# Hybrid attention layers: weighted sums with the exponentials as stationary operand, gates among the neighbourhood heads, earlier loads for scan and Fourier mixer

## The chip, the cores and the metric

One core of a Trainium2 chip runs the whole program. The metric is device microseconds of one execution. Three runs of the kernel before took 3113.3, 3114.28 and 3123.29 us, median 3114.28 us.

## The reference

Two layers act on 1024 latent tokens and 256 context tokens of width 1024. A layer normalises and modulates the tokens, projects them by one matrix `w_in`, feeds four head groups in parallel, joins their outputs (256 channels each) by one matrix `w_out`, and ends with a squared-ReLU MLP. The second layer gives no context output. The parts that matter here:

```python
# grouped-query attention (4 query heads, 2 key heads, 64 channels); scores and sums in float32
s = einsum('bqkgd,bskd->bkgqs', q, k_all)         # k_all: latent and context keys
o = einsum('bkgqs,bskd->bqkgd', softmax(s), v_all)
# neighbourhood attention (4 heads): an 8 x 16 window of the 16 x 64 grid with a bias, plus all context keys
p = softmax(concat([q.k_window + bias, q.k_ctx]))
o = p_window @ v_window + p_ctx @ v_ctx
# S5: two complex diagonal scans per group of 16 channels, then
t = gelu(y);  o = t * sigmoid(t @ w_glu)
# Fourier mixer: real part of a 2-D DFT over positions and channels, then
o = f @ w_fnet + b_fnet
y = concat([oa, ob, on, od]) @ w_out
```

## The kernel before, in words

Tokens stand in ten tiles of 128. Large projections are exact to float32 by three products of rounded halves (`mm3`, lines 159 to 161: high by high, high by low, low by high); scores and weighted sums are float32 products. The program is written in stages as Python generators, and `weave`, `every` and `along` interleave their steps; a scheduler then puts instructions into each engine's queue by priority, which `early` raises for side work. So the order in a queue follows from the steps' places and priorities. Each queue is worked in order.

A layer's attention (`attention`) runs over units: six for grouped-query attention (two key heads; four, four and two query tiles; the last are context queries and are absent in layer 1), then four neighbourhood heads. `gqa_main` and `na_main` take one tile of 128 keys after the other: PE makes scores (L641, L772), DVE adds the bias in neighbourhood heads (L153), ACT takes the exponential `e`, and two steps later `pv` (L611) makes the weighted sums. There v, with a column of ones, is the stationary operand (128 keys by 65 columns), and up to 512 queries of `e` stream past it; the result is 65 rows by queries, whose last row is the softmax denominator. At the end of a unit ACT copies the 64 rows to `oraw` and DVE copies the denominator row to `rden`; `finish` sends that row by DMA to a tile of 128 partitions (L665), takes the reciprocal (L671), sends it through DRAM (L672) back to 64 partitions (L675), and POOL multiplies `oraw` by it into `o`.

Among these steps runs side work: every second step one of the S5 scan `s5_scan` during the grouped-query units, every third step one of the Fourier mixer `fnet` during the neighbourhood heads, and `attn_prep` (queries, keys and maxima of the next unit). `s5_scan` loads three tables per group in the same step as the first product that reads them (L1268), and in its second group loads `t0` and copies it whole to `tm`, which ACT does in one instruction.

After the heads comes `w_out`. It loads eight 128-row units of `w_out` into `raw` tiles, splits each into `wh` and `wl`, splits the attention output into `oh` and `ol`, and makes products `wh,oh`. In its first steps it also runs `glu`, the gates of S5 (L1334 to L1369: loads of the scan's output `yt` and of `gwr`, GELU on DVE, ACT and POOL, products `th,gwh`, and a sigmoid times the input).

## Time and profile before

| | |
|---|---|
| median of three runs | 3114.28 us |
| profiled execution, its own time | 3110.25 us |
| its span, first to last instruction | 3108.5 us |
| mean granted TensorE clock | 0.968 |
| busy: PE, PEld, DVE, ACT, POOL | 93%, 76%, 53%, 35%, 30% |
| chain that ended last | PE 56%, DVE 6%, DMA 5% |
| `mm3` products of the w_in and MLP stages, largest group | 519.7 us (1536 products) |
| one of the weighted sums' groups (L611, `e,zg`) | 170.7 us (336 records) |

A clock of 1.0 is 2.4 GHz, and 0.5 is 1.2 GHz. Attention begins at 299.8 us in layer 0 and at 1956.6 us in layer 1 (first scores); its neighbourhood heads begin at 501.7 and 2160.3 us. The first product of the output projection stands at 670.43 and 2297.50 us. PE, the engine that is busy most, sets the pace nearly everywhere, so PE's waits and PE's own instructions are what to read; a float32 product shows as two records in the trace, each with its own weight load on PEld.

### The profile page before, as it was taken

How to read it: one execution, taken by the hardware profiler on the slowest of the kernel's cores; microseconds unless marked ns; L12 is line 12 of the kernel's file. 1: busy time of each engine (PE TensorE's matmuls, PEld its weight loads, DVE VectorE, ACT ScalarE, POOL GpSimd, SP SyncE). 2: the span in 40 equal slices, each digit the busy share in tenths (PEclk: the TensorE clock that was granted, in tenths of full speed). 3: DMA queues.
4: the chain of work that ended last, by engine and by line, in shares of the span. 5: the costliest groups of instructions: out<-in, count | busy, mean ns of one | idle time of the engine just before them, and what ended most of it. 6: DMA issues, size and time to landing. Idle time of an engine off the chain costs nothing.

```text
span 3108.5 us, 38660 instructions
## 1 busy us (share of the span) xinstructions
PE 2899.1 (93%) x14816; PEld 2361.5 (76%) x14816; DVE 1640.4 (53%) x2240; ACT 1094.7 (35%) x1856; POOL 938.2 (30%) x847
## 2 busy tenths in 40 slices
PE   6999897979999999999999989788979999999998
PEld 3788554658888889898988788554657888888887
DVE  3475564664775544754554785464755233443334
ACT  3443653553322222422222344454553222122212
POOL 2563222235521112511122563122335111111113
PEclk8999898979999999999999999998989999999999
DMA  7544425342544322432333443525343211111113
GB/s 280 171 129 108 95 72 152 84 158 82 176 149 130 128 90 82 158 120 95 116 102 109 152 141 104 94 72 147 96 156 113 64 55 41 54 41 55 54 41 109
DMA packets 244190, 340.04 MB, mean 109 GB/s; under 512 B 52037, under 2 KB 188581, under 8 KB 244005
## 3 DMA queue, kind: packets, MB, share of 16 engines
q1 hardware_dynamic: 244004, 337.57, 35.9%
q8 instruction: 116, 1.90, 0.3%
q14 instruction: 70, 0.57, 0.1%
HBM read 283.78 MB, written 53.62 MB: 109 GB/s over the span
## 4 chain that ended last, share of the span: by engine, by line
PE 56%; DVE 6%; DMA 5%; issue 3%; POOL 3%; ACT 2%; SPq 0%; DVEq 0%; POOLq 0%; ACTq 0%
PE ps L159 17%; PE ps L161 17%; PE ps L160 17%; PE ps L611 2%; DMA raw<-in_w_ada_dram 1%; DVE wl L150 1%; DVE y L153 1%; PE ps L772 1%; POOL rs L215 1%; PE ps L641 1%; DMA raw<-in_w_mlp_dram 0%; DVE acc L292 0%; DMA s5u<-u 0%; DVE y L1390 0%; DMA kd<-zn 0%
## 5 line engine op out<-in xcount | busy, mean ns | idle before, releaser
L159 PE MATMUL ps<-mh,wh 128*128 128x320 f32 (+1 forms) x1536 | 519.7, 338 | 11.5 <-DVE y L153 6.4
L147 ACT ACTIVATE wh<-raw 128x1024 fp32r<-128x1024 f32 x234 | 242.9, 1056 | 787.6 <-PE ps L161 551.9
L161 PE MATMUL ps<-mh,wl 128*128 128x320 f32 (+1 forms) x1536 | 517.5, 337 | 1.1 <-DVE wl L150 1.1
L160 PE MATMUL ps<-ml,wh 128*128 128x320 f32 (+1 forms) x1536 | 517.6, 337 | 0.0
L159 PE MATMUL ps<-wh,hidh 128*128 128x512 f32 x1152 | 451.5, 392 | 1.4 <-DVE y L153 1.4
L161 PE MATMUL ps<-wh,hidl 128*128 128x512 f32 x1152 | 447.8, 390 | 1.8 <-POOL hidl L150 1.8
L160 PE MATMUL ps<-wl,hidh 128*128 128x512 f32 x1152 | 449.3, 390 | 0.0
L153 DVE TENSOR_TENSOR y<-ps,y 128x1024 f32<-128x1024 f32 (+1 forms) x253 | 306.4, 1218 | 261.7 <-PE ps L161 261.7
L150 POOL TENSOR_TENSOR hidl<-r,hidh 128x640 fp32r<-128x640 f32 (+1 forms) x128 | 188.9, 1476 | 672.7 <-DVE r L153 672.7
L150 DVE TENSOR_TENSOR wl<-raw,wh 128x1024 fp32r<-128x1024 f32 x188 | 289.1, 1550 | 163.3 <-ACT wh L147 158.9
L159 PEld LDWEIGHTS ps<-mh,wh 128*128 128x128 f32 x1536 | 290.3, 189 | 37.4 <-issue 7.3
L161 PEld LDWEIGHTS ps<-mh,wl 128*128 128x128 f32 x1536 | 289.8, 189 | 22.3 <-DVE wl L150 2.3
L160 PEld LDWEIGHTS ps<-ml,wh 128*128 128x128 f32 x1536 | 290.3, 189 | 20.8
L150 POOL TENSOR_TENSOR wl<-raw,wh 128x1024 fp32r<-128x1024 f32 x48 | 120.3, 2507 | 471.6 <-ACT wh L147 471.5
L159 PEld LDWEIGHTS ps<-wh,hidh 128*128 128x128 f32 x1152 | 216.6, 188 | 52.2 <-issue 6.2
L161 PEld LDWEIGHTS ps<-wh,hidl 128*128 128x128 f32 x1152 | 216.5, 188 | 48.1 <-POOL hidl L150 2.7
L160 PEld LDWEIGHTS ps<-wl,hidh 128*128 128x128 f32 x1152 | 216.7, 188 | 43.2
L153 DVE TENSOR_TENSOR r<-r 128x640 f32<-128x640 f32 (+1 forms) x128 | 96.6, 755 | 241.7 <-ACT hidh L1488 241.6
L1486 ACT ACTIVATE r<-ps 128x640 f32<-128x640 f32 (+1 forms) x128 | 82.2, 644 | 367.9 <-PE ps L161 360.2
L611 PE MATMUL ps<-e,zg 128*65 128x512 f32 (+1 forms) x336 | 170.7, 598 | 3.8 <-DVE rden L653 2.8
L292 DVE SCALAR_TENSOR_TENSOR acc<-raw,cst,acc 128x1024 f32<-128x1024 f32 x70 | 101.5, 1474 | 136.1 <-DMA raw<-in_w_ada_dram 136.1
L159 PE MATMUL ps<-hh,wh 128*128 128x320 f32 (+1 forms) x480 | 151.5, 316 | 2.7 <-ACT vst L147 2.7
(427 smaller groups left out, 5328.1 us busy)
## 6 DMA issues: line engine op xcount, KB each, us to landing
raw<-in_w_mlp_dram SPq DMA_DIRECT2D x192, 512.0 KB
raw<-in_w_ada_dram SPq DMA_DIRECT2D x96, 512.0 KB
raw<-in_w_in_dram SPq DMA_DIRECT2D x28, 512.0 KB
x<-x SPq DMA_DIRECT2D x26, 512.0 KB
x<-h SPq DMA_DIRECT2D x18, 512.0 KB
x<-in_x_dram SPq DMA_DIRECT2D x16, 512.0 KB
raw<-in_w_out_dram SPq DMA_DIRECT2D x16, 512.0 KB
bq<-in_na_bq_dram SPq DMA_DIRECT2D x8, 800.0 KB
```

What stands on the lines that cost most here:

```text
L147: self.nc.scalar.activation(out, in_, AF.Copy, scale=scale)
L150: (eng or self.nc.vector).tensor_tensor(out=out, in0=a, in1=b, op=OP.subtract)
L153: (eng or self.nc.vector).tensor_tensor(out=out, in0=a, in1=b, op=op)
L159: self.nc.tensor.matmul(ps, ah, bh, start=start and i == 0, stop=False)
L160: self.nc.tensor.matmul(ps, ah, bl, start=False, stop=False)
L161: self.nc.tensor.matmul(ps, al, bh, start=False, stop=stop and i == n - 1)
L215: nc.gpsimd.tensor_tensor(out=r, in0=r, in1=self.mhalf.to_broadcast([128, n]), op=OP.pow)
L292: nc.vector.scalar_tensor_tensor(acc[c], x, col, acc[c], op0=OP.mult, op1=OP.add)
L611: self.nc.tensor.matmul(po[0:65], vf[:, kt, :], e, start=start, stop=stop)
L641: nc.tensor.matmul(ps, kk[:, ks], qq[:, hs], start=kk is k1, stop=kk is k2)
L772: nc.tensor.matmul(ps, kk[:, ks], qq[:, x:y], start=kk is k1, stop=kk is k2)
L1486: nc.scalar.activation(r.rearrange("p (b n) -> p b n", b=nb), ps[:, :nb, :w], AF.Relu)
```

## The change

**Weighted sums.** `e` becomes the stationary operand, 128 keys by 128 queries, and the 65 columns of v stream past it; the result is 128 queries by 65. Each query tile of each key tile is a product of its own: 1,088 of them in the program, where there were 304 products. `sums` first clears the two result banks with one-row bf16 products of zeros, 36 in all. The denominator now stands beside its sums on the same partition, so `divide` takes a reciprocal and multiplies on DVE; `finish` transposes the quotients on PE (72 transposes) and copies them into `o`. The copies `oraw` and `rden`, the three DMAs of each of 18 units, the way through DRAM and POOL's multiplications are gone. In neighbourhood heads, tiles that begin at an odd row of the grid are padded by 64 columns of zeros (POOL), and the sums of the context queries stand after the first key tile instead of at the head's end.

**Gates.** `glu` is chained behind `fnet` as side work among the neighbourhood heads, where a step of it now comes every 5/2 steps; `w_out` loads its eight units in one go and takes them in the order 0, 1, 2, 3, 6, 7, 4, 5.

**Loads.** `s5_scan` loads its tables one group ahead and `t0` three steps ahead of the first group, and copies `tm` in four parts; `fnet` loads four `u0` tiles at its start.

```diff
+        self.zero = c.tile([1, 512], BF16, name="zero")
+        nc.vector.memset(self.zero, 0.0)
...
-    def pv(self, queue, vf, kt, parts, start, stop):
+    def sums(self, n):
+
+
+        po = self.ps2(tag="pO")
+        for b in range(2):
+            self.nc.tensor.matmul(po[:, b * 512:b * 512 + n * 65], self.zero[:, :128], self.zero[:, :n * 65],
+                                  start=True, stop=False)
+        return po
+
+    def pv(self, queue, vf, kt, po, parts, end=()):
 
 
         def whole():
-            for po, e in parts:
-                self.nc.tensor.matmul(po[0:65], vf[:, kt, :], e, start=start, stop=stop)
+            for (b, c), e in parts:
+                self.nc.tensor.matmul(po[:, b * 512 + c * 65:b * 512 + c * 65 + 65], e, vf[:, kt, :],
+                                      start=False, stop=(b, c) in end)
         queue.append((2, whole))
...
+        po = self.sums(u["n"])
...
-            self.pv(queue, vf, kt, [(po[:, h * 512:h * 512 + w], e[:, h * w:(h + 1) * w]) for h in range(2)],
-                          kt == kts[0], kt == NT - 1)
+            self.pv(queue, vf, kt, po, [((h, t), e[:, h * w + t * 128:h * w + (t + 1) * 128])
+                                        for h in range(2) for t in range(u["n"])],
+                    [(h, u["n"] - 1) for h in range(2)] if kt == NT - 1 else ())
...
-        tags = (("oraw2", 256), ("rden2", 512)) if u["b"] == 2 else (("oraw", TOK), ("rden", TOK))
-        oraw, rden = (st["fp"].tile([128, n], F32, tag=tag, bufs=1, name=tag) for tag, n in tags)
-        for h in range(2):
-            self.copy(oraw[64 * h:64 * h + 64, :w], po[0:64, h * 512:h * 512 + w])
-        nc.vector.tensor_copy(rden[0:1, :2 * w].rearrange("p (h n) -> p h n", h=2),
...
+        n = u["n"]
+        on = st["fp"].tile([128, 4, 2, 64], F32, tag="on", bufs=2, name="on")
+        self.divide(st, po, on[:, :n].rearrange("p t h d -> p h t d"), n)
+        st["fin"] = self.finish(lambda t: on[:, t].rearrange("p h d -> p (h d)"), n, o, u["j"], u["t0"])
...
+    def divide(self, st, po, dst, n):
+
+        src = po.rearrange("p (b c) -> p b c", b=2)[:, :, :n * 65].rearrange("p b (t d) -> p b t d", d=65)
+        r = st["fp"].tile([128, 2, 5], F32, tag="rt", bufs=2, name="rt")[:, :, :n]
+        self.nc.vector.reciprocal(r, src[:, :, :, 64])
+        self.tt(dst, src[:, :, :, 0:64], r[:, :, :, None].to_broadcast([128, 2, n, 64]), OP.mult)
+
+    def finish(self, src, n, o, kt, t0):
+
+        yield
+        yield
+        for i0 in range(0, n, 4):
+            m = min(4, n - i0)
+            ps = self.ps1()
+            for i in range(m):
+                self.nc.tensor.transpose(ps[:, i * 128:(i + 1) * 128], src(i0 + i), self.ident)
+            for i, k, dst in self.put_o(o, kt, (t0 + i0) * 128, m * 128):
+                self.copy(dst, ps[:, i:i + k])
...
+        po = self.sums(nq // 256)
...
+            r0 = ra - ra % 2
+            e = st["pg"].tile([128, 1024], F32, tag="e", bufs=4, name="e")[:, :(rb - r0) * 64]
+            if r0 < ra:
+                nc.gpsimd.memset(e[:, 0:64], 0.0)
...
-            cols = [(po[:, x:y], slice(x - ra * 64, y - ra * 64)) for x, y in pieces]
-            self.pv(queue, s["vf"], kt, [(x, e[:, c]) for x, c in cols], i == 0, i == 9)
-            yield
+            self.pv(queue, s["vf"], kt, po, [((t % 2, t // 2), e[:, t * 128 - r0 * 64:(t + 1) * 128 - r0 * 64])
+                                             for t in range(r0 // 2, rb // 2)], [(0, 3), (1, 3)] if i == 9 else ())
+            yield
+            if i == 0 and nq > NLAT:
...
+                for c in range(2):
+                    ks = slice(1024 + c * 128, 1152 + c * 128)
+                    nc.tensor.matmul(ps[:, c, :], k1[:, ks], q1[:, 1024:1280], start=True, stop=False)
+                    nc.tensor.matmul(ps[:, c, :], k2[:, ks], q2[:, 1024:1280], start=False, stop=True)
...
+        if h % 2 == 0:
+            st["on"] = st["fp"].tile([128, NT, 2, 64], F32, tag="onn", bufs=1, name="onn")
+        on = st["on"]
+        n = nq // 256
+        self.divide(st, po, on[:, :2 * n, h % 2].rearrange("p (c b) d -> p b c d", b=2), n)
+        st["fin"] = iter(())
+        if h % 2:
+            st["fin"] = self.finish(lambda t: on[:, t].rearrange("p h d -> p (h d)"), 2 * n, o, 4 + h // 2, 0)
...
-                side, every = fnet, 3
+                side, every = fnet, 5 / 2
...
+        done = 0
         for i, x in enumerate(main):
-            if i % n == n - 1:
+            if int((i + 1) / n) > done:
+                done += 1
                 next(other, None)
             yield x
...
+            us = {}
+            for t0 in (0, 512, 256, 768):
+                us[t0] = p.tile([128, 516], F32R, tag="wh", bufs=4, name="u0")[:, :512].bitcast(F32)
+                nc.sync.dma_start(us[t0].rearrange("p (m t) -> p m t", m=2), uf[:, :, t0:t0 + 256])
...
+                if t0 not in us:
+                    nc.sync.dma_start(u, uf[:, :, t0:t0 + 256])
...
-        def front(g):
-            v, cs, sn = (p.tile([128, 2, w], F32, tag=n, bufs=2, name=n) for n, w in (("v", 128), ("cs", 160), ("sn", 160)))
-            for t, n in ((v, "v"), (cs, "cs"), (sn, "sn")):
+        def ins(g):
+
+            ts = [p.tile([128, 2, w], F32, tag=n, bufs=2, name=n) for n, w in (("v", 128), ("cs", 160), ("sn", 160))]
+            for t, n in zip(ts, ("v", "cs", "sn")):
                 nc.sync.dma_start(t, dr[n][:, g])
+            return ts
+
+        def front(g, v, cs, sn):
...
+        tabs = ins(0)
+        yield
+
+        t0 = p.tile([128, 16, 128], F32, name="s5t0")
+        for j in range(8):
+            nc.sync.dma_start(t0[j * 16:(j + 1) * 16], dr["e"][:, :, (7 - j) * 16:(7 - j) * 16 + 128])
+        yield
+        yield
         for g in range(16):
-            st = (g, front(g))
+            now, tabs = tabs, ins(g + 1) if g < 15 else None
+            st = (g, front(g, *now))
...
-            if g == 1:
-
-                t0 = p.tile([128, 16, 128], F32, name="s5t0")
-                for j in range(8):
-                    nc.sync.dma_start(t0[j * 16:(j + 1) * 16], dr["e"][:, :, (7 - j) * 16:(7 - j) * 16 + 128])
-                self.copy(tm.rearrange("p g (h j) -> p g j h", j=8), t0.rearrange("p g (j h) -> p g j h", j=8))
+            if g % 4 == 1:
+
+                gs = slice(g - 1, g + 3)
+                self.copy(tm[:, gs].rearrange("p g (h j) -> p g j h", j=8), t0[:, gs].rearrange("p g (j h) -> p g j h", j=8))
...
+    def glu(self, l, o):
+
+        with self.pool(f"glu{l}", "right") as p:
+            yield from self.gates(p, l, o)
+
+    def gates(self, p, l, o):
...
-        w, order = {}, (0, 1, 4, 5, 6, 7, 2, 3)
+        w, order = {}, (0, 1, 2, 3, 6, 7, 4, 5)
...
-        for i in range(4):
+        for i in range(KT):
             load(i)
-        glu = self.glu(gp, l, o)
-        next(glu)
-        for i in range(4, KT):
-            load(i)
-        glu = self.early(glu, 300)
         rows = later = hh = first = None
         for t in range(nt):
-            if t % 2 == 0:
-                next(glu, None)
...
-            for ks in (slice(0, 2), slice(4, 8), slice(2, 4)) if t < 2 else (slice(0, 8),):
+            for ks in (slice(0, 2), slice(2, 4), slice(6, 8), slice(4, 6)) if t < 2 else (slice(0, 8),):
...
-                for _ in glu:
-                    pass
-                gp.release()
...
-            self.attention(l, st, o, self.early(self.fnet(l, o), 100))
+            self.attention(l, st, o, self.early(itertools.chain(self.fnet(l, o), self.glu(l, o)), 100))
```

Line numbers of `mm3` move by 2, and others by 2 to 33. Three places of the queues, before and after:

PE at the start of attention in layer 0, before: `ql` and `qhh` are transposes of query tiles of a next unit (L520), L641 is a score, and L1268 the scan's first product.

```order
L520 MATMUL ps<-identr,ql 128x128 x8
L1268 MATMUL ps<-s5u,v 128x160 x2
L520 MATMUL ps<-identr,qhh 128x128 x4
L641 MATMUL ps<-g0q_2779,g0k_2775 128x512 x2
L584 MATMUL ps<-g0k_2774,g1q_3289 128x512 x4
L641 MATMUL ps<-g0q_2778,g0k_2774 128x512
```

The same place after the change (L522, L653; L622 is the new weighted sum). The scan's first product is no longer among them.

```order
L586 MATMUL ps<-g0k_2776,g0q_2780 128x512 x5
L593 MATMUL ps<-g0k_2776,g0q_2780 128x256 x8
L522 MATMUL ps<-identr,ql 128x128 x8
L522 MATMUL ps<-identr,qhh 128x128 x4
L653 MATMUL ps<-g0q_2781,g0k_2777 128x512 x2
L586 MATMUL ps<-g0k_2776,g1q_3290 128x512 x4
L653 MATMUL ps<-g0q_2780,g0k_2776 128x512
L653 MATMUL ps<-g0q_2781,g0k_2777 128x512
L622 MATMUL ps<-zg,e 128x65 x4
```

It now stands 48 rows behind `ql` instead of one: scores, maxima and sums of several key tiles come before it.

SP, which issues the loads, at the end of layer 0's attention, before: L1334 and L1336 are the gates' loads, L665 to L675 the denominators' way, L194 rows of the modulation, L169 the units of `w_out`.

```order
L1334 DMA yt_6218<-s5y_149 128x1280
L1334 DMA yt_6220<-s5y_149 128x1280
L665 DMA rt<-rden 128x1x10
L1336 DMA gwr<-in_w_s_glu_dram 128x2x256
L194 DMA rg<-mod_2_82 128x1024
L194 DMA ra<-mod_4_84 128x1024
L194 DMA rb<-mod_3_83 128x1024
L672 DMA den_6160<-rt 128x10
L675 DMA rden<-den_6160 64x1280
L169 DMA raw<-in_w_out_dram 128x1024 x8
```

The same place after the change, where `n1q` (L755) is a row of the last head's preparation.

```order
L1367 DMA yt_6346<-s5y_151 128x1280
L1367 DMA yt_6348<-s5y_151 128x1280
L1369 DMA gwr<-in_w_s_glu_dram 128x2x256
L755 DMA n1q_5213<-nmt 1x10x128
L196 DMA rg<-mod_2_84 128x1024
L196 DMA ra<-mod_4_86 128x1024
L196 DMA rb<-mod_3_85 128x1024
L171 DMA raw<-in_w_out_dram 128x1024 x8
```

The eight loads of `w_out` no longer stand behind two DMAs of the last head's denominators, but still behind `rg`, `ra` and `rb`.

PE at the end of layer 0's attention, before: the last sums of the last head and of its context queries, then the gates' products.

```order
L611 MATMUL ps<-e,nvf_4966 65x320
L611 MATMUL ps<-e,nvf_4966 65x512 x2
L611 MATMUL ps<-ec,nvf_4966 65x256 x2
L159 MATMUL ps<-th,gwh 128x256 x2
L160 MATMUL ps<-tl,gwh 128x256
L161 MATMUL ps<-th,gwl 128x256
L160 MATMUL ps<-tl,gwh 128x256
```

Thirty-three more rows of gates' products follow, and then the first products of the output projection. After the change no gate stands behind the last scores (L778); `onn` are the transposes of the quotients (L683).

```order
L622 MATMUL ps<-nvf_5214,e 128x65 x4
L778 MATMUL ps<-n1q_5212,n1k_5208 128x512
L778 MATMUL ps<-n1q_5213,n1k_5209 128x512
L622 MATMUL ps<-nvf_5214,e 128x65 x4
L778 MATMUL ps<-n1q_5212,n1k_5208 128x512
L778 MATMUL ps<-n1q_5213,n1k_5209 128x512
L622 MATMUL ps<-nvf_5214,e 128x65 x11
L683 MATMUL ps<-ident,onn 128x128 x10
L161 MATMUL ps<-wh,oh 128x512 x2
L162 MATMUL ps<-wl,oh 128x512
```

The first products of the output projection follow on the last head's transposes.

## Rows read from the trace of the kernel before

**Rows 1.** Windows: stretch, length, busy us (x instructions) per engine, PEclk, DMA share, GB/s

```profile
300.00:500.00 200.00, 173.13 (x707) 105.42 (x706) 116.80 (x225) 112.10 (x214) 51.74 (x84) 0.94 0.46 100
500.00:639.00 139.00, 120.08 (x570) 79.00 (x570) 80.22 (x179) 64.10 (x132) 34.11 (x29) 0.91 0.37 104
639.00:670.00 31.00, 13.81 (x44) 10.23 (x45) 20.61 (x48) 20.91 (x50) 10.83 (x10) 0.53 0.38 138
...
1957.00:2160.00 203.00, 165.95 (x645) 99.71 (x645) 107.08 (x217) 105.74 (x198) 51.66 (x84) 0.92 0.50 109
2160.00:2272.00 112.00, 105.56 (x487) 67.32 (x486) 72.25 (x161) 54.39 (x107) 27.72 (x26) 0.96 0.36 104
2272.00:2297.00 25.00, 9.92 (x35) 8.07 (x35) 17.10 (x40) 17.74 (x43) 9.85 (x10) 0.58 0.36 126
```

**Rows 2.** Waits of PE, 300 to 645 us: us in total, times, longest

```profile
PE ps L159 <- ACT uh L147: 7.7, 1, 7.7
...
PE ps L1268 <- DMA v<-s5v: 7.5, 1, 7.5
```

**Rows 3.** Waits of PE, 1957 to 2000 us

```profile
PE ps L641 <- ACT e L642: 8.4, 2, 6.7
PE ps L1268 <- DMA x<-s5x: 4.9, 1, 4.9
```

**Rows 4.** Timeline of layer 1: start, us, engine, line, operation; in brackets idle before

```profile
1987.40 3.86 ACT L147 ACTIVATE s5tm<-s5t 128x2048 f32<-128x2048 f32 x1 [5.61 <-DMA v<-s5v]
```

**Rows 5.** Windows: the stretches at the lower clock around the scan's first products

```profile
306.00:327.00 21.00, 10.49 (x32) 6.90 (x33) 8.17 (x17) 6.23 (x10) 0.91 (x2) 0.51 1.21 144
...
1961.00:1996.00 35.00, 21.17 (x65) 12.26 (x66) 13.09 (x26) 16.64 (x25) 5.14 (x7) 0.80 0.92 115
```

**Rows 6.** Timeline of layer 0, end of attention to the first output product

```profile
633.54 0.49 DVE L153 TENSOR_TENSOR e<-ps,nbt 128x320 f32<-128x320 f32 x1 [0.57 <-PE ps L772]
...
638.79 1.01 ACT L147 ACTIVATE oraw<-ps 64x1024 f32<-64x1024 f32 x1 [1.66 <-PE ps L611]
...
652.92 2.07 SPq L169 DMA_DIRECT2D raw<-in_w_out_dram  x4
...
670.43 1.05 PE L159 MATMUL ps<-wh,oh 128*128 128x512 f32 x2
```

**Rows 7.** Timeline of layer 1, the same place

```profile
2272.24 1.02 ACT L147 ACTIVATE oraw<-ps 64x1024 f32<-64x1024 f32 x1 [2.38 <-PE ps L611]
...
2284.08 2.00 SPq L169 DMA_DIRECT2D raw<-in_w_out_dram  x4
...
2297.50 1.05 PE L159 MATMUL ps<-wh,oh 128*128 128x512 f32 x2
```

**Rows 8.** Groups by form, PE: weights*columns, moved, xcount | busy, mean ns

```profile
L611 PE MATMUL ps<-e,zg 128*65 128x512 f32 x320 | 165.7, 605 | 2.9 <-DVE rden L653 1.8 <-ACT e L642 1.1
...
L611 PE MATMUL ps<-e,nvf 128*65 128x512 f32 x144 | 75.1, 616 | 4.6 <-ACT e L776 4.6
```

**Rows 9.** Timeline of PE: f32 products that follow each other, and one alone

```profile
429.50 0.71 PE L1301 MATMUL ps<-z,x 128*128 128x160 f32 x4
...
430.51 1.02 PE L611 MATMUL ps<-e,zg 128*65 128x512 f32 x2
...
493.01 0.59 PE L611 MATMUL ps<-e,zg 128*65 128x512 f32 x1
```

**Rows 10.** Timeline: weight loads of 128 columns with few columns moved

```profile
295.17 0.46 PEld L520 LDWEIGHTS ps<-identr,qhh 128*128 128x128 f32 x4
...
494.25 0.53 PEld L732 LDWEIGHTS ps<-n0k,n0q 128*128 128x128 f32 x4
...
2224.95 0.19 PEld L732 LDWEIGHTS ps<-n0k,n0q 128*128 128x128 f32 x1 [0.29 <-DVE e L153]
```

**Rows 11.** Timeline: one-pass products of 256 columns in a row

```profile
635.80 0.28 PE L790 MATMUL ps<-n1q,n1k 128*128 128x256 f32 x1
...
635.92 0.28 PE L791 MATMUL ps<-n1q,n1k 128*128 128x256 f32 x1
```

More of the change, by code (lines that the diff above doesn't have):

```diff
@@ L657, in gqa_main @@
-        yield
-    def finish(self, st, oraw, rden, rows, w, nh, o, kt, t0):
-        nc, n = self.nc, w * nh
-        c = n // 128
-        r = st["fp"].tile([128, 10], F32, tag="rt", bufs=2, name="rt")[:, :c]
-        nc.sync.dma_start(r, rden[0:1, :n].rearrange("a (p c) -> a p c", c=c))
-        self.dn += 1
-        d = self.dram.tile([128, c], F32, name=f"den{self.dn}")
+        n = u["n"]
+        on = st["fp"].tile([128, 4, 2, 64], F32, tag="on", bufs=2, name="on")
+        self.divide(st, po, on[:, :n].rearrange("p t h d -> p h t d"), n)
@@ L668, in finish @@
+    def finish(self, src, n, o, kt, t0):
         yield
         yield
-        yield
-        nc.vector.reciprocal(r, r)
-        nc.sync.dma_start(d, r)
-        yield
-        yield
-        nc.sync.dma_start(rden[rows, :w], bass.AP(tensor=d.tensor, offset=d.offset,
-                                                  ap=([[w, 2]] if nh > 1 else []) + [[0, 64], [1, w]]))
-        yield
-        yield
-        yield
-        for i, m, dst in self.put_o(o, kt, t0, w):
-            self.tt(dst[rows], oraw[rows, i:i + m], rden[rows, i:i + m], OP.mult, nc.gpsimd)
+        for i0 in range(0, n, 4):
[5 more added lines that the diff above has]
+                self.copy(dst, ps[:, i:i + k])
@@ L769, in na_main @@
                 ps = self.ps1(tag="s1")[:, :y - x]
-                ee = e[:, x - ra * 64:y - ra * 64]
+                ee = e[:, x - r0 * 64:y - r0 * 64]
                 for kk, qq in ((k1, q1), (k2, q2)):
@@ L801, in na_main @@
-        st["fin"] = self.finish(st, oraw, rden, hs, nq, 1, o, 4 + h // 2, 0)
-        next(st["fin"])
+            if i == 0 and nq > NLAT:
+                ps = self.ps1(tag="s1").rearrange("p (b n) -> p b n", b=2)
+                for c in range(2):
+                    ks = slice(1024 + c * 128, 1152 + c * 128)
+                    nc.tensor.matmul(ps[:, c, :], k1[:, ks], q1[:, 1024:1280], start=True, stop=False)
+                    nc.tensor.matmul(ps[:, c, :], k2[:, ks], q2[:, 1024:1280], start=False, stop=True)
+                e = st["pg"].tile([128, 1024], F32, tag="e", bufs=4, name="ec")[:, :512]
+                nc.scalar.activation(e.rearrange("p (b n) -> p b n", b=2), ps, AF.Exp)
+                yield
+                self.due(queue)
+                for c in range(2):
+                    self.pv(queue, s["vf"], 8 + c, po, [((t, 4), e[:, c * 256 + t * 128:c * 256 + (t + 1) * 128])
+                                                        for t in range(2)])
+                yield
@@ L826, in attention @@
         up = self.open(f"up{l}")
-        for n, w in (("oraw", TOK), ("rden", TOK), ("oraw2", 256), ("rden2", 512)):
-            up.tile([128, w], F32, tag=n, bufs=1, name=n)
+        for n, w, b in (("on", 512, 2), ("onn", TOK, 1), ("rt", 10, 2)):
+            up.tile([128, w], F32, tag=n, bufs=b, name=n)
         pg = self.open(f"attG{l}")
@@ L1393, in epi_rear, with w_out @@
         return h
-    def w_out(self, p, l, o, gp, hp=None):
+    def w_out(self, p, l, o, hp=None):
         a = self.a
@@ L1642, in run @@
             with self.pool(f"wo{l}", "right") as p:
-                *h2, later, first = self.w_out(p, l, o, self.open(f"glu{l}"), last)
+                *h2, later, first = self.w_out(p, l, o, last)
             self.own = {}
```

30 lines of the change are left out of this document (1 added, 29 removed).

## Prediction

> **What bounds the kernel now.** I read the busy shares first: PE is busy 93% of the span, so a gain must shorten PE's own work or its waits. Then I cut the span into windows by stage [rows 1]. In the dense parts PE is busy 85 to 94%; between the end of attention and the output projection it is busy 13.81 of 31 us in layer 0 and 9.92 of 25 us in layer 1, at a clock of 0.53 and 0.58. Third, I asked what PE waits for where attention starts. The reader is to see four waits: 7.7 us for `uh`, which is the Fourier mixer's first, 7.5 us for the scan's table `v` in layer 0 [rows 2], 4.9 us for the scan's `x`, and 6.7 us for an `e` in layer 1 [rows 3]. The last is no slow exponential: ACT spent 3.86 us on the copy of `tm` there, after 5.61 us idle for a load [rows 4], and the exponential stands behind it. Two stretches there run at a lower clock, 0.51 over 21 us and 0.80 over 35 us [rows 5]. Last, I followed both ends of attention in order of time [rows 6, 7].
>
> All terms are in us, for both layers together, against the profiled execution's own 3110.25.
>
> **The weighted sums, by PE.** Before: by the program the sums make 608 records, and their columns add up to those of 536 records of 512; most are the 320 and 144 records of 512 columns in the list of groups [rows 8]. Their busy means of 605 and 616 ns hold overlap, so I take the pitch: two records end to end take 1.02, one alone 0.59, so a following one costs 0.43 [rows 9], and 536 x 0.43 = 230.5. After: 1,088 products are 2,176 records, each with a weight load of 128 columns and 65 columns to stream. No row shows exactly that. The streaming alone would be 0.43 x 65/512 = 0.055. The loads alone: four in a row take 0.53 and one 0.19, so 0.113 each for spaced ones; another four take 0.46, or 0.09 each [rows 10]. Is a load hidden behind its neighbour's stream? Four float32 records of 160 columns, each with its load of 128 columns, take 0.71 [rows 9], at most 0.18 each, where 0.133 of streaming plus 0.11 of load would make 0.24: it is hidden. So the longer of the two sets the pace: 0.11, the value nearest to spaced loads of this size; 2,176 x 0.11 = 239.4. The sum changes by +8.9; the lower end, 0.09, gives -34.7, the upper, 0.113 + 0.055 = 0.168 with nothing hidden, +135. So the sums cost about the same as before. What changes is how PE spends the time: loading for most of it.
>
> The Trainium skill (TensorE: Matmul & The Clock Gate, The mechanism) says that a weight load overlaps products in flight only where their row group differs. Here all loads use all 128 rows, so by it the pitch would be load plus stream, 0.168, and the sums would cost 126 more than in my forecast (an estimate by the page's rule from the trace's prices). The 160-column records speak against it.
>
> **New PE work.** 36 zeroings of up to 325 one-pass columns at 0.12 each, the pitch of 256 one-pass columns [rows 11]: +4.3. 72 transposes at 0.11, a load of 128 columns: +7.9. The gates' 108 products of 256 columns now stand in attention, no longer in the ends' idle time: 108 x 0.12 = +13.0. Removed on other engines are `oraw`, `rden`, POOL's multiplications and 54 DMAs; none but those at the ends is waited for by PE in the windows, so they count nothing here. Their replacement `divide` reads the result banks on DVE; the sums of the next unit go to other banks, which covers it. Were that cover gone, a unit would wait about 2 us, 36 in all.
>
> **Waits removed.** The table `v`, `x` and `u0` are loaded ahead, and by the order of PE's queue the scan's first product comes several key tiles later. `tm` is copied in four parts, so no exponential stands behind more than a quarter of 3.86. I let all four waits go: -(7.7 + 7.5 + 4.9 + 6.7) = -26.8. Late next would be the seven other loads that the scan issues in the same stretch, for which I leave 2 either way.
>
> **The lower clock after these waits.** In the first stretch 10.49 of PE work ran at about half speed, worth 5.2 at full; in the second 0.80 means 14 of 35 at half, at a busy share of 0.6, worth 4.2 [rows 5]. Without the waits the clock need not fall: -9.4. Below, 0.
>
> **The ends of attention.** Before, the first output product came 31.6 after the last head's sums (670.43 less 638.79) in layer 0 and 25.3 in layer 1 (2297.50 less 2272.24) [rows 6, 7]. From the issue of the `w_out` loads to that product it was 17.5 and 13.4. After the change these loads stand behind `rg`, whose tile is freed by the last local key tile's `e`, at 634.03 in layer 0, 4.8 before the sums end; three issues of about 0.5 come between. At the old 17.5 the product comes 14 after the sums. But most of those 17.5 went with engines that also worked on gates, and these are gone: a load, a cast of 1 and a subtraction of 1.5 come to 5 after. I take 10, the middle, in both layers: -(31.6 - 10) - (25.3 - 10) = -36.9, between -46.9 and -28.9.
>
> **Gates among the heads.** The gates' work on DVE and ACT moves with them. At the ends DVE was busy 20.61 + 17.10 = 37.7 and ACT 20.91 + 17.74 = 38.6 [rows 1]. In layer 0's heads DVE had 80.22 of 139 and would have about 100, in layer 1's 72.25 of 112 and then about 89 [rows 1]; the bias additions stand in the same DVE queue, and PE waits for their `e`. There is room on average, not everywhere; I take 6 of the 37.7, between 0 and 37.7.
>
> **Sum.** 8.9 + 4.3 + 7.9 + 13.0 - 26.8 - 9.4 - 36.9 + 6 = -33.0, which gives 3077.2. The median of the runs shown stands 4.0 above that execution, so the forecast is **3081**. A measurement of this kernel can tell about 0.3% (9) from no change; 3105 and 3124 are the bounds.
>
> **Rivals.**
>
> *Weight loads pace at 0.09.* The four query transposes' loads do so [rows 10], and a float32 load may stand closer when nothing else moves. The sums are then 2,176 x 0.02 = 43.5 cheaper: 3037.5. Against it: most spaced rows show 0.11. Chance 0.13.
>
> *Gates are not hidden.* Three steps to two and a half is a denser stream of side work, and DVE's queue is worked in order: a gate's step before a bias addition holds that `e`, and PE behind it. Its price is up to the whole 37.7 in place of 6: 3113, no change. For it: DVE at 0.58 of layer 0's heads already, at 0.65 of layer 1's. Against it: PE then has other rows to do, as the gates' own products. Chance 0.12.
>
> *The clock falls in attention.* The granted clock in this trace fell where PE streamed little: 0.51, 0.53 and 0.58 in stretches with PE busy half the time or less [rows 1, 5]. In the new sums PE streams 0.055 of each 0.11, by loads for the rest. PE works 565 in the four windows of attention [rows 1]; each tenth of it that falls to 1.2 GHz adds 57. From 43 more than my sum, that is from 7.5% of this work on, the kernel is slower than before by more than can be told; at a fifth it is 3081 + 113 = 3194. Against it: the scan's and transposes' short records stand in windows at 0.91 to 0.96 now. Chance 0.07.
>
> *Weight loads are not hidden.* 0.113 + 0.055 = 0.168 in place of 0.11 for 2,176 records: +126, 3207. This is the place where the page's rule above would come true. Against it stand the 160-column records. Chance 0.03.
>
> *The change doesn't do what it says*: gates or loads end where they were because the scheduler ranks them so. The queues' order shows that gates stand among the heads and `w_out` behind `rg`, so I give it no chance of its own; that `rg` waits for the last head anyhow is in the bound of 14.
>
> **How the numbers follow.** The forecast has 0.65; its own bounds are 3063 to 3105 (ends -10 to +8, clock up to +9.4, gates -6 to +14, loads 2 either way, not all at once). The range holds it, the cheap loads and the lower half of unhidden gates: 3034 to 3111. Out of it stay the clock (0.07), serial loads (0.03) and a few hundredths above and below. Faster: 0.65 less 0.02, 0.13, and 0.03 of the gates' case: 0.79. Same: the rest of the gates' case and the forecast's edge, 0.10. Slower: 0.11, being clock, serial loads and a hundredth of the gates.
>
> **What would show it.** The list by form should give L622 a pitch near 0.11 end to end, at full clock in the windows. PE's waits should have no `v`, `uh` or `x` above 2; the first output product should stand about 10 behind the last head's sums, with PE busy in the windows of the heads by some 7 more each. A pitch of 0.16 or a clock under 0.85 in attention would make the prediction wrong on the slow side; a pitch of 0.09 on the fast side. If PE's waits for `e` in the heads grow by over 15, the gates are not hidden.

## The result, and the profile after

The changed kernel took 3083.41 us, median of four runs (3064.83 to 3099.34), beside 3117.28 for the kernel before: ratio 0.9882, 95% interval 0.9858 to 0.9905. The forecast was 3081, or 33 less than before; measured are 34 less. The sum held. Its terms did not all hold, and the errors cancelled.

The profiled execution took 3064.83 (span 3062.3, before 3108.5), so it is the fastest of the four, and 18.6 under their median. The four went in two pairs: 3064.83 and 3070.35 at a mean granted clock of 0.972, 3096.47 and 3099.34 at 0.964. That pairing turned out to be the main finding, below.

The windows by stage, cut at the first scores, the first score of the neighbourhood heads, the last sums and the first output product, answer to [rows 1]. Columns: stretch, length, busy us (x instructions) of PE, PEld, DVE, ACT, POOL, PEclk, DMA share, GB/s.

```profile
303.00:505.00 202.00, 185.78 (x1237) 166.71 (x1235) 116.23 (x232) 110.16 (x214) 47.32 (x80) 0.91 0.45 97
505.00:641.00 136.00, 131.20 (x957) 120.51 (x956) 96.97 (x232) 80.14 (x181) 34.77 (x45) 0.95 0.37 103
641.00:647.00 6.00, 2.31 (x12) 1.54 (x11) 3.82 (x10) 2.40 (x7) 0.99 (x1) 0.65 1.01 337
1936.00:2125.00 189.00, 169.29 (x1151) 153.42 (x1150) 108.08 (x217) 102.43 (x197) 49.41 (x81) 0.93 0.48 105
2125.00:2246.00 121.00, 117.31 (x836) 105.04 (x835) 85.01 (x204) 69.89 (x156) 27.92 (x41) 0.96 0.36 103
2246.00:2252.00 6.00, 2.25 (x11) 1.71 (x10) 3.67 (x10) 2.20 (x7) 1.04 (x1) 0.59 1.01 345
```

The reader is to see the two stretches of 6 us, which were 27 and 25, and DVE in the heads at 97 of 136 and 85 of 121, near the 100 and 89 that the forecast gave. The first layer's grouped-query stage is as long as before (202), although its wait for `v` is gone.

What took its place shows in PE's waits, layer 0 and then layer 1 (us in total, times, longest), which answer to [rows 2, 3]:

```profile
PE ps L653 <- ACT e L654: 9.7, 3, 7.7
...
PE ps L161 <- DVE gl L152: 2.2, 1, 2.2
```

```profile
PE ps L653 <- ACT e L654: 11.3, 3, 10.2
PE ps L752 <- DVE nmr L743: 3.9, 1, 3.9
```

and in ACT's timeline there, which answers to [rows 4]:

```profile
330.09 3.87 ACT L149 ACTIVATE s5tm<-s5t 128x512 f32<-128x512 f32 x4 [10.63 <-DMA cs<-s5cs]
333.75 1.11 ACT L654 ACTIVATE e<-ps 128x512 f32<-128x512 f32 x2
...
1965.10 3.87 ACT L149 ACTIVATE s5tm<-s5t 128x512 f32<-128x512 f32 x4 [10.43 <-DMA v<-s5v]
```

`x4` is the point: the four copies stand together, in front of the exponentials, and ACT is idle for over 10 us until their table has landed. (The first of them waits for all eight loads of `t0`; `cs`, which the profile names, is a later load on one of the same semaphores.) Layer 0 before, with the table's loads on SP and the one copy, and then the same loads after:

```profile
318.19 5.23 SPq L1315 DMA_DIRECT2D s5t<-s5e  x8
...
330.09 3.94 ACT L147 ACTIVATE s5tm<-s5t 128x2048 f32<-128x2048 f32 x1 [2.05 <-DMA v<-s5v]
```

```profile
318.42 5.29 SPq L1334 DMA_DIRECT2D s5t<-s5e  x8
```

So the table's loads hardly moved, and the copying begins at 330.09 in both kernels. Counted from the first scores, the loads are issued 3 to 4 us earlier in either layer, and the copying begins 3.2 and 1.4 us earlier. ACT has 10 instructions of attention in front of the copies in layer 0, where it had 13, and has done them sooner, so it waits 10.63 us there instead of 2.05.

The ends of attention, layer 0 (the loads' issue, the last sums, the first cast, the first output product) and layer 1, answer to [rows 6, 7]:

```profile
638.19 2.28 SPq L171 DMA_DIRECT2D raw<-in_w_out_dram  x4
...
640.82 0.39 PE L622 MATMUL ps<-nvf,e 128*128 128x65 f32 x2
...
646.01 1.04 POOL L182 CAST wh<-raw 128x1024 fp32r<-128x1024 f32 x1 [13.33 <-DMA raw<-in_w_out_dram]
...
647.10 1.22 PE L161 MATMUL ps<-wh,oh 128*128 128x512 f32 x2 [2.62 <-POOL wh L182]
...
2245.78 0.50 PE L622 MATMUL ps<-nvf,e 128*128 128x65 f32 x3
...
2252.02 1.22 PE L161 MATMUL ps<-wh,oh 128*128 128x512 f32 x2 [2.75 <-POOL wh L182]
```

The product comes 5.9 and 5.7 us behind the last sums, in layer 0 8.9 behind the loads' issue. The sums, in the list by form and in the timeline, answer to [rows 8, 9]:

```profile
L622 PE MATMUL ps<-zg,e 128*128 128x65 f32 x1312 | 179.1, 273 | 0.4 <-ACT e L654 0.4
L622 PE MATMUL ps<-nvf,e 128*128 128x65 f32 x832 | 109.9, 274 | 0.3 <-ACT e L782 0.2
```

```profile
560.02 0.78 PE L622 MATMUL ps<-nvf,e 128*128 128x65 f32 x6
...
564.31 1.00 PE L622 MATMUL ps<-nvf,e 128*128 128x65 f32 x8
```

Two more records make 0.22 more: a pitch of 0.11.

**One account for all kernels.** I divide the time of the six stretches into three. *Idle* is the sum of PE's waits, that of the first output product among them. *Work* is each record's end less the end before it, less the wait, at full clock. *Clock excess* is what the same work took longer because it stood at 1.2 GHz, counted as half of the working time at that clock (a sum's record that follows another measures 0.213 us there and 0.112 at full clock). As a check by hand: a window of 136 us at a mean clock of 0.95 has 2 x 0.05 = 10% at 1.2 GHz, some 14 us, of which half, about 7, is excess. All are of the profiled executions.

| kernel | median us | idle | excess | work | of it sums | excess, NA heads 0 and 1 |
|---|---|---|---|---|---|---|
| before | 3117 | 121.6 | 42.0 | 548.0 | 233.0 | 8.5, 4.7 |
| changed | 3083.4 | 52.0 | 36.7 | 571.7 | 229.2 | 6.8, 4.9 |
| changed, again | 3083.9 | 58.5 | 30.8 | 572.2 | 229.4 | 5.1, 4.0 |
| tm_pool | 3066.0 | 37.4 | 53.5 | 569.6 | 228.8 | 20.2, 9.0 |
| loads_undone | 3074.4 | 52.9 | 34.5 | 572.4 | 228.8 | 12.3, 2.9 |
| pv_undone | 3113.8 | 123.0 | 46.7 | 549.8 | 234.5 | 15.6, 7.4 |
| pv_only | 3105.6 | 74.9 | 59.4 | 562.9 | 228.1 | 7.1, 22.8 |
| pv_only_102 | 3080.1 | 73.0 | 30.2 | 567.6 | 239.7 | 3.6, 5.1 |
| glu_undone | 3119.6 | 73.4 | 87.3 | 561.2 | 227.4 | 35.0, 24.8 |
| glu_undone_102 | 3077.2 | 74.4 | 33.4 | 565.0 | 239.4 | 4.9, 8.6 |
| pv32 | 3165.7 | 55.3 | 168.2 | 559.8 | 215.8 | 53.5, 45.1 |
| pv102 | 3063.7 | 63.8 | 27.3 | 575.1 | 240.1 | 1.7, 8.2 |
| pv102_tm | 3033.4 | 41.9 | 21.1 | 574.4 | 240.0 | 2.6, 5.0 |
| pv128_tm | 3040.0 | 40.7 | 10.1 | 579.8 | 246.1 | 0.0, 5.8 |

The kernel before had medians of 3115.7 to 3119.9 beside these. A profiled execution can lie off its median by up to 19: that of the changed kernel is 19 under it, those of glu_undone, pv32 and pv102 are 10 to 14 above theirs.

### The profile page after: what moved, and what is told of

Its sections match the earlier page's. It is cut to its first block, busy times and chain, and to the rows that moved or that the text cites. A ratio compares the mean times of both kernels' runs of the same rounds, so it can differ in the third digit from the quotient of the medians.

```text
span 3062.3 us, 41885 instructions
## 1 busy us (share of the span) xinstructions
PE 2920.0 (95%) x16492; PEld 2539.9 (83%) x16492; DVE 1632.1 (53%) x2245; ACT 1084.1 (35%) x1858; POOL 901.7 (29%) x849
## 5 line engine op out<-in xcount | busy, mean ns | idle before, releaser
L622 PEld LDWEIGHTS ps<-zg,e 128*128 128x128 f32 x1312 | 186.1, 199 | 15.8 <-ACT e L654 0.8
L622 PE MATMUL ps<-zg,e 128*128 128x65 f32 x1312 | 179.1, 273 | 0.4 <-ACT e L654 0.4
```

Source lines behind the costliest of these rows:

```text
L622: self.nc.tensor.matmul(po[:, b * 512 + c * 65:b * 512 + c * 65 + 65], e, vf[:, kt, :], start=False, stop=(b, c) in end)
```

## Experiments

**1. The copies into `tm` on POOL (tm_pool).**

```diff
-                self.copy(tm[:, gs].rearrange("p g (h j) -> p g j h", j=8), t0[:, gs].rearrange("p g (j h) -> p g j h", j=8))
+                self.nc.gpsimd.tensor_copy(tm[:, gs].rearrange("p g (h j) -> p g j h", j=8), t0[:, gs].rearrange("p g (j h) -> p g j h", j=8))
```

> The four copies into tm go from ACT to POOL; nothing else is changed against the changed kernel. Theory (the two waits of 7.7 and 10.2 us for an exponential at the start of each layer's attention are ACT's queue standing behind these copies, which wait for the table's load): both waits fall under 3 us, PE idles some 14 to 18 us less, and the time falls by 12 to 25 us against the changed kernel. Rival (PE would wait there anyhow, for the scan's own tables or for exponentials): the waits come back under other names and the time falls by less than 5 us.

Median 3065.97, ratio to before 0.9845 (0.9811 to 0.9879), 17 under the changed kernel. The waits are as the theory had them: those for `e` in grouped-query attention fell to 1.9 and 1.0, and idle by 14.6. The time is in the theory's range by the medians, but the intervals of the two ratios overlap; it is clear of noise only with 102 columns, where the same edit is worth 30 (experiment 9). POOL's timeline shows the wait where it hurts nobody, and the windows of the heads (columns as above) show why the profiled execution gained nothing although the median did:

```profile
333.89 4.16 POOL L1345 COPY s5tm<-s5t 128x512 f32<-128x512 f32 x4 [20.95 <-DMA v<-s5v]
```

```profile
502.00:651.00 149.00, 144.04 (x956) 131.75 (x954) 98.20 (x232) 80.23 (x181) 34.04 (x45) 0.86 0.33 93
...
2123.00:2248.00 125.00, 119.72 (x836) 108.62 (x835) 85.03 (x203) 69.74 (x155) 28.38 (x41) 0.92 0.33 96
```

The first layer's heads, which this edit does not touch, ran at 0.86 here and at 0.95 in the changed kernel, with PE busy 97% of the time.

**2. The new sums alone (pv_only).** The kernel before with the change's `sums`, `pv`, `divide`, `finish`, `gqa_main` and `na_main`:

```diff
-    def pv(self, queue, vf, kt, parts, start, stop):
+    def sums(self, n):
...
+    def pv(self, queue, vf, kt, po, parts, end=()):
...
+    def divide(self, st, po, dst, n):
```

> The kernel before with the weighted sums, divisions and transposes of the change alone. Theory (the sums cost PE the same in both orientations, their pitch is that of a weight load, 0.11 us; what is won is waits for exponentials behind ACT's and DVE's copies, and part of the ends, since the w_out loads no longer stand behind the denominators' DMAs): PE's share of the sums 229 to 240 us, time 5 to 25 us under the kernel before. Rival (the orientation carries most of the gain, by waits): 30 us or more under it. Second rival (it costs time, by the added zeroings and transposes of 12 us): 0 to 15 us above it.

3105.56, ratio 0.9967 (0.9952 to 0.9982), 10 under the kernel before: the theory, with the sums at 228.1. Idle fell by 47, work rose by 15, and the clock took 17 back.

**3. The gates back in the output projection (glu_undone).**

```diff
-            self.attention(l, st, o, self.early(itertools.chain(self.fnet(l, o), self.glu(l, o)), 100))
+            self.attention(l, st, o, self.early(self.fnet(l, o), 100))
...
-                side, every = fnet, 5 / 2
+                side, every = fnet, 3
...
-        w, order = {}, (0, 1, 2, 3, 6, 7, 4, 5)
+        w, order = {}, (0, 1, 4, 5, 6, 7, 2, 3)
```

> The changed kernel with the gates back in the output projection, the old order of the w_out units, and the Fourier mixer at every third step. Theory (the two ends of attention are worth about 41 us, of which the gates' 13 us of products and the friction in the heads are given back): the first output product stands 20 us or more behind the last sums again, the neighbourhood heads get 10 to 15 us shorter in each layer, and the time is 15 to 30 us above the changed kernel. Rival (the ends are short because the denominators' DMAs are gone, not because the gates are): the first output product stays within 10 us of the last sums, and the time is within 5 us of the changed kernel's.

3119.61, ratio 1.0021 (0.9996 to 1.0047): 36 above the changed kernel, all of its gain, and more than the 15 to 30 expected. The ends are 18.1 and 16.5, not over 20, so some 18 of the 41 us there come with the new sums, whose denominators need no DMA; the new sums alone (experiment 2) leave 17.1 and 16.7. And the heads got longer, not shorter, by 21 and 12 us: their work fell by 9 and 10, but the clock fell too.

```profile
513.00:670.00 157.00, 150.47 (x897) 137.44 (x896) 82.06 (x179) 60.68 (x126) 26.26 (x35) 0.78 0.33 99
...
2168.00:2302.00 134.00, 128.65 (x793) 115.69 (x791) 75.08 (x163) 54.28 (x111) 20.86 (x33) 0.80 0.33 95
```

**4. The loads as before (loads_undone).** `s5_scan` and `fnet` of the kernel before:

```diff
-        tabs = ins(0)
...
-            us = {}
```

> The changed kernel with the scan's and the Fourier mixer's loads as they were before. Theory (the scan's loads arrive as fast as the DMA queues carry them in either order, the copy of tm began at 330.09 us both times, so only the Fourier mixer's 5.5 us were won): PE waits 7 us for v and some 7 for x and the exponential in layer 1 again, but no longer 7.7 and 10.2 for exponentials; the time is 0 to 10 us above the changed kernel. Rival (the forecast's own term): 27 us above it.

3074.43, ratio 0.9869 (0.9852 to 0.9886): 9 under the changed kernel, so the loads ahead were worth nothing; the theory had 0 to 10 above. In layer 0 PE waits 8.6 for `cs` in place of 7.7 for an `e`, in layer 1 for an `e` and `cs` in place of 10.2 for an `e`:

```profile
PE ps L1279 <- DMA cs<-s5cs: 8.6, 1, 8.6
PE ps L653 <- ACT e L654: 1.7, 2, 1.4
```

```profile
PE ps L653 <- ACT e L654: 9.9, 2, 8.1
PE ps L1279 <- DMA cs<-s5cs: 2.7, 1, 2.7
```

That 9 is within what the changed kernel's own runs differ by.

**5. The changed kernel again (after_again).** No edit.

> The changed kernel itself, to be set beside the three others. Theory (in the new sums PE streams for only half of the time, and the granted clock falls now in one part of attention, now in another, from execution to execution): its times spread over 1% or more, 3060 to 3100 us, against 0.4% of the kernel before, and executions differ by their mean clock. Rival (the two early high values were a disturbance): its times lie within 0.3% of 3065 us.

3071.05 to 3087.3, median 3083.88, ratio 0.9882 (0.9860 to 0.9905). Its two runs at a clock of 0.971 took 3071 and 3073, its three at 0.964 to 0.967 took 3084 to 3087. Time goes with the clock from execution to execution. The spread of 1% did not come in these five alone: it is 0.5% here, and 1.1% in the first four. The rival's 3065 did not come either.

**6 and 7. Fewer and more columns streamed (pv32, pv102).** The columns that pass each stationary tile are changed, at the same count of records; with 102, the places of the results and the zeroed stretch widen with them.

```diff
-                self.nc.tensor.matmul(po[:, b * 512 + c * 65:b * 512 + c * 65 + 65], e, vf[:, kt, :],
+                self.nc.tensor.matmul(po[:, b * 512 + c * 65 + 33:b * 512 + c * 65 + 65], e, vf[:, kt, 33:65],
```

> The changed kernel with only the last 32 of the 65 columns of v and ones streamed in each weighted sum; the other 33 channels are left out of the sums. At full clock the theory of the weight load as pace has the pitch stay at 0.11 us; the theory that loads and streams add up has it fall by 0.028, 60 us in all. If the clock falls because PE streams too little, the half-clock part of attention grows and the time rises by 10 to 60 us against the changed kernel although less is computed; if the clock does not follow the streaming, the time stays within 10 us.

```diff
-                self.nc.tensor.matmul(po[:, b * 512 + c * 65:b * 512 + c * 65 + 65], e, vf[:, kt, :],
+                self.nc.tensor.matmul(po[:, b * 512 + c * 102:b * 512 + c * 102 + 102], e, vf(kt),
```

> The changed kernel with 102 columns streamed in each weighted sum, the 65 wanted and 37 neighbours that nothing reads. At full clock the theory has the pitch stay at 0.11 us, since 102 columns stream in 0.086; the zeroings get 3 us longer. If the clock falls because PE streams too little, the half-clock part of attention shrinks, the spread of the times narrows to 0.5%, and the median falls by 5 to 25 us against the changed kernel. Rival (the clock does not follow the streaming): median and spread stay, within 6 us. Second rival (loads and streams add up): 68 us slower.

With 32 columns: 3165.69, ratio 1.0149 (1.0130 to 1.0167), 82 *slower* than with 65, at less work and beyond the 10 to 60 expected. With 102: 3063.65, ratio 0.9834 (0.9815 to 0.9854), 20 faster, at more work. The windows of 32 columns and then of 102:

```profile
306.00:542.00 236.00, 215.01 (x1239) 193.35 (x1239) 116.95 (x233) 110.78 (x214) 48.50 (x81) 0.78 0.39 85
542.00:717.00 175.00, 173.62 (x957) 159.98 (x957) 98.97 (x232) 81.07 (x181) 32.95 (x44) 0.70 0.27 77
2001.00:2203.00 202.00, 181.45 (x1150) 164.41 (x1149) 107.58 (x216) 102.60 (x197) 50.01 (x81) 0.86 0.45 98
2203.00:2362.00 159.00, 153.60 (x839) 139.61 (x837) 87.40 (x205) 71.38 (x156) 27.77 (x41) 0.70 0.28 80
```

```profile
306.00:510.00 204.00, 185.02 (x1237) 166.48 (x1236) 114.88 (x232) 110.04 (x213) 47.19 (x81) 0.92 0.43 93
510.00:647.00 137.00, 129.91 (x961) 117.09 (x960) 96.34 (x234) 80.02 (x183) 35.20 (x46) 0.99 0.38 108
1941.00:2128.00 187.00, 165.69 (x1151) 150.22 (x1150) 107.63 (x215) 102.31 (x196) 49.71 (x83) 0.95 0.47 104
2128.00:2255.00 127.00, 119.48 (x838) 107.24 (x837) 87.36 (x205) 69.40 (x156) 28.92 (x41) 0.92 0.35 101
```

The second line is the one to keep: PE is busy 173.62 of 175 us and its clock is 0.70; with 102 columns it is busy less and runs at 0.99. At full clock the median pitch of records that follow each other was 0.112 us with 32, 65 and 102 columns, so the load sets it. Idle differs little, and is the smaller with 32 (55.3 and 63.8); the clock excess differs much (168.2 and 27.3). The spread, which I expected to fall to 0.5%, was 0.4%.

**8. The old sums in the changed kernel (pv_undone).** `pv`, `gqa_main`, `na_main` and `finish` of the kernel before:

```diff
-        po = self.sums(u["n"])
+        po = self.ps2(tag="pO")
```

> The changed kernel with the weighted sums and the denominators' way as before. Theory (the sums cost PE the same either way; the new ones save the denominators' DMAs at the ends and waits behind copies, and pay by the clock): the clock excess in the neighbourhood heads falls to some 10 us for both layers, the spread to under 0.5%, the ends are 10 us longer in each layer since the last head's division still goes through DRAM, and the median lies between 15 us above and 10 us below the changed kernel's. Rival (the orientation carries the gain): 25 us or more above.

3113.77, ratio 0.9986 (0.9973 to 0.9999), 30 above the changed kernel. My theory fell, the rival's time holds, though not by PE's work in the sums (234.5 against 229.2). But neither part carries the gain by itself: gates and loads without the new sums, which is this run, win some 4 us, the new sums alone won 10 (experiment 2), together they win 34. The four windows of attention take 659 us before, 692 here, where the gates stand among heads with the old sums, and 649 in the changed kernel. Idle is 123.0 against 52.0, of which 28 and 8 stand at the ends. The clock excess in the heads did not fall to 10; it is 23.0, against 11.7. Of PE's waits in the four windows, those for an `e` sum to 41.0 against 22.3, those for `mx` of the next head's preparation to 11.2 against next to nothing; the longest in layer 0 and 1:

```profile
PE ps L652 <- ACT e L653: 15.7, 5, 12.8
PE ps L622 <- ACT e L794: 5.8, 5, 3.9
```

```profile
PE ps L652 <- ACT e L653: 14.1, 4, 12.5
```

The two longest, 12.8 and 12.5, stand behind the copies of `tm` once more, for which ACT is idle here still longer:

```profile
332.15 3.87 ACT L149 ACTIVATE s5tm<-s5t 128x512 f32<-128x512 f32 x4 [12.51 <-DMA v<-s5v]
...
1998.53 2.03 ACT L149 ACTIVATE s5tm<-s5t 128x512 f32<-128x512 f32 x2 [13.98 <-DMA s5t<-s5e]
```

Without these two, and without the 7.7 and 10.2 of the changed kernel, the waits for an `e` are 15.7 against 4.4. ACT's `oraw` copies and DVE's `rden` copies stand in the same queues as the exponentials' and maxima's steps, so they may be what these shorter waits are for; which of them it is was not tried alone and stays open.

**9 to 11. The combinations.** Both edits that helped (pv102_tm); the gates back, with 102 columns (glu_undone_102); the new sums alone, with 102 columns (pv_only_102). Each is the earlier edit and this one:

```diff
-            self.nc.tensor.matmul(po[:, b * 512:b * 512 + n * 65], self.zero[:, :128], self.zero[:, :n * 65],
+            self.nc.tensor.matmul(po[:, b * 512:b * 512 + n * 102], self.zero[:, :128], self.zero[:, :n * 102],
...
+        vr = s["vf"].rearrange("p t c -> p (t c)")
+        vf = lambda kt: vr[:, kt * 65:kt * 65 + 102]
```

> The changed kernel with 102 columns streamed per weighted sum and the copies into tm on POOL, that is both edits that helped. Theory (they act on different losses, the first on the clock and the second on PE's wait behind ACT's queue): PE idles some 15 us less than in the changed kernel, the clock excess in attention is below 25 us, and the median is 25 to 45 us under the changed kernel's, 3040 to 3060. Rival (the time saved in one is lost in the other, as the clock falls where waits vanish): not faster than the better of the two, 3063.

> The changed kernel with the gates back in the output projection, and 102 columns streamed per weighted sum. Theory (with the gates back, the clock fell in the neighbourhood heads, since the gates' products of 256 columns no longer stood among the sums that stream little; the clock excess there was 60 us in the profile): with 102 columns this excess falls to 25 us or less, and the time is 20 to 45 us under that of the kernel with the gates back and 65 columns (3119.6). Rival (the heads are slow without the gates for another reason): within 10 us of it.

> The kernel before with the new weighted sums alone, and 102 columns streamed per sum. Theory (the new sums alone won only 10 us because the clock excess in attention rose from 42 to 59 us): with 102 columns the excess is 35 us or less and the time 12 to 30 us under that with 65 columns (3105.6). Rival (the clock has no part in it): within 8 us of it.

pv102_tm took 3033.43, ratio 0.9733 (0.9712 to 0.9754): 50 under the changed kernel, more than the theory's 25 to 45, and the best of all. The losses are separate ones. PE idles 10 less than in the changed kernel, where 15 were expected. glu_undone_102 took 3077.24, ratio 0.9874 (0.9848 to 0.9900), 42 under 65 columns; its heads now run at

```profile
506.00:637.00 131.00, 124.64 (x901) 111.82 (x899) 80.21 (x181) 60.77 (x128) 25.63 (x36) 0.96 0.38 112
...
2127.00:2247.00 120.00, 113.34 (x791) 101.83 (x789) 75.57 (x163) 54.07 (x112) 21.71 (x33) 0.92 0.36 106
```

pv_only_102 took 3080.10, ratio 0.9880 (0.9854 to 0.9905), 25 under 65 columns. So the new sums alone, with more columns, win as much as the whole change did. And what the gates did among the heads was more than leaving the ends: at 65 columns the excess in the heads is 59.8 without them there and 11.7 with them. That it is their products of 256 columns that keep the clock up fits this, but was not tried apart from the mixer's pace, which the same edit changes. With 102 columns the gates' place is worth 14 (3077.2 against 3063.7; the intervals of the ratios overlap a little) where it was worth 36.

**12. 128 columns (pv128_tm).**

```diff
+        S = 128 if n < 5 else 102
```

> As the kernel with 102 columns and the copies on POOL (3033.4), but 128 columns streamed wherever at most four query tiles share a bank; the first layer's neighbourhood heads keep 102. A record of 128 columns streams in 0.43 x 128/512 = 0.108 us, as long as its weight load of 0.112 takes. Theory (the load sets the pace, so up to some 130 columns cost nothing at full clock, and a clock excess of 21 us is left to win from): the sums stay within 12 us, and the median is 0 to 15 us under 3033.4. Rival (pitches of load and stream that are alike disturb each other, or the rest of the excess follows PE's waits alone): within 5 us of 3033.4 or up to 20 us above.

3039.98 (3030.79 to 3042.58), ratio 0.9743 (0.9726 to 0.9760), 7 above pv102_tm: not the theory's 0 to 15 under, and within the rival's range. Excess fell to 10.1 in the profile, work rose by 5, and the sums by 6; but the profile is of the fastest of five executions, and the medians don't tell the two kernels apart (the ratios' intervals overlap). Whether 128 columns are better or worse than 102 stays open.

## Why the prediction was right, and where it was not

**The sums by PE: right.** The load sets the pace: 0.112 was measured, 0.11 taken. They take 229.2 after 233.0; the forecast was 239.4 after 230.5, too high by 10, because a sum that follows a product of 256 or 512 columns has its load covered and costs only 0.057, its stream. The rival of loads that are not hidden falls. By the sentence that the prediction cites from the Trainium skill (TensorE: Matmul & The Clock Gate, The mechanism) it would be 0.168; the same section also lets a load go ahead into a background weight buffer, and the measurement agrees with that.

**PE's work as a whole: right in the sum, in part by luck.** +34.1 forecast, +32.6 measured in the four windows of attention (536.8 to 569.4). The sums took 3.8 less, not 8.9 more. The zeroings took 6.0 and the gates 13.8, where 4.3 and 13.0 were taken; the transposes took 8.7, 6.5 of it in these windows, where 7.9 were taken. And the products that the change leaves alone, scores above all, took some 10 more among the new sums, for which the forecast has no term.

**Waits removed: the step "I let all four waits go" failed.** `v`, `x` and the wait for `uh` did go (2.2 is left, for `gl`). But the step "`tm` is copied in four parts, so no exponential stands behind more than a quarter of 3.86" was read from the diff: in ACT's queue the four stand together, and they wait for a table whose loads did not come ahead as far (issued at 318.42 in layer 0, before at 318.19; the first copy began at 330.09 in both kernels). New waits of 7.7 and 10.2 came. Undoing all the loads cost nothing (experiment 4), where this term gave 26.8.

**What made up for it: smaller waits that I had left at nothing.** Idle in the four windows fell by 46.9 (91.3 to 44.4); of the four waits named, net of what replaced them, come only 26.8 - 7.7 - 10.2 - 2.2 = 6.7. The step "none but those at the ends is waited for by PE, so they count nothing" (of `oraw`, `rden` and POOL's multiplications) is the one that failed. The rows before spoke against it: in the four windows PE's waits for `rden` come to 5.2, and those for `mx`, whose steps share a queue with `rden`, to 13.8. Not all of the 40 is shown to come with the orientation: beside the named waits and what replaced them, the new sums alone remove 29 (experiment 2), and taking them out of the changed kernel puts back 46 (experiment 8). Which copy was waited for is not shown.

**The ends: right, mis-sized by 4.** 36.9 forecast, 41.2 measured from the last sums: 6 us instead of 10 in each layer. (In layer 0 the forecast counted from 638.79, when ACT began to copy the last head; the sums of the context queries ended 4.3 later.) Experiment 3 divides it: about 18 by the new sums, 23 by the gates.

**The clock: failed.** I took 9.4 off; the excess in the four windows went from 30.7 to 34.8. The rival "the clock falls in attention" had 0.07. It came true, to some degree, in a part of the executions: 30 us lie between the pairs of the changed kernel's first four runs. Its reason was right, as pv32 and pv102 show. Without the gates among the heads it decides: in experiment 3 there are 87.3 of excess and, with 23 of the ends given back, no gain at all.

**Gates among the heads: right.** No new wait above 2.4 in the heads names DVE's or ACT's gate steps; idle there went from 27.1 to 8.5.

**The sum.** In the profiled executions the four windows gave 10.2 (32.6 more work, 46.9 less idle, 4.1 more excess), the ends 41.2, and the rest of the program took 4.9 more, 3.2 of it before the first scores, of which the cause stays open: the span fell by 46, where 33 were forecast. Too little by 26 on the waits (20.8 with the friction of 6, against 46.9) stands against too much by 13.5 on the clock. That the medians differ by 34, as forecast, is because the typical execution of the changed kernel is 19 slower than the profiled one, at a lower clock: a part of the agreement is luck.

## What to carry to other kernels

Making the small operand stream past the large one cost PE no time here, where the weight load hides the stream, and it spares every copy and DMA that a result lying the wrong way needs; count the short waits that go with these too (29 to 46 us here, none of them over 6). But then look at the granted clock: if it falls among the new products, stream idle columns that the load hides. Wider products put between may serve as well, which is argued here and not shown. Parts of a change can need each other, so try each alone and all but each. And read a queue's order for every instruction that the forecast rests on: a step cut into four in the source may stand as one in the queue, and a load that is moved ahead in the source gains only what it moves ahead in its own queue.

## What the hardware did that was not expected

PE's clock fell while PE was busy 99% of a stretch (0.70, busy 173.62 of 175 us), and adding columns that nothing reads made the kernel 20 us faster, or 50 us with the other edit. The Trainium skill (TensorE: Matmul & The Clock Gate, HAM oscillation — how this bites in real kernels) puts such losses down to gaps in which PE is idle, and advises a loop with fewer waits or padding the thin dimension. The waits agree in part: stretches at the lower clock stand around them before (0.51 from 306 to 327 us [rows 5]) and after (0.59 in the same stretch). But the table's pv32 has 8.5 us less idle time than pv102 and an excess that is larger by 141, so here it is what PE streams, not whether it waits.
